# A Strassen-type output projection: one of seven split products taken as plain fp32, and its overwriting sums moved later

## The chip, the core and the metric

The kernel runs on one core of a Trainium2 chip. TensorE (PE in the profile) multiplies, VectorE (DVE), ScalarE (ACT) and GpSimd (POOL) prepare operands and empty the accumulators, SyncE (SP) issues most transfers. The metric is device time in microseconds (us) of one execution.

## The reference, cut to what matters

The reference is a decoder trunk of two layers on a sequence of 1024 vectors of 1024 features: sparse attention and a SwiGLU in layer 0, a gated MLP over chunks and a SwiGLU in layer 1. Each of the four sub-layers ends in a projection back to 1024 features that is added to the residual stream, and these four second projections are all that the change touches:

```python
return o @ w_o                                   # attention, inner size 1024
return y @ w_out                                 # gated MLP, inner size 2048
return (jax.nn.silu(h @ w_gate) * (h @ w_up)) @ w_down   # SwiGLU, inner size 2816
x = x + g1[:, None, :] * y                       # the gated residual add
```

All of it is fp32, and the comparison asks for nearly fp32 accuracy.

## The kernel before, in words

**Products.** TensorE is fed mostly with a reduced fp32 format (`float32r`). To keep accuracy every operand is split into a high part (a cast on ACT) and a low part (the difference, a subtraction on DVE or POOL), and `mm3` makes three matmuls of them: high times high, high times low, low times high (lines 176, 177 and 178). A few early projections are not split; they call `PE.matmul` on plain fp32 tiles (line 463).

**The second projection.** `out_win` computes it by Winograd's form of Strassen's scheme, seven products in place of eight. The inner dimension is cut in pieces (`[4]` for attention, `[4, 4]` for the gated MLP, `[4, 4, 3]` for each SwiGLU; a number is how many 128-wide blocks one half has). For a piece, the activations are loaded as `graw` tiles (`"1"` and `"2"`: quadrants b11, b12 and b21, b22) and the weights as `wraw` tiles (`"A"`: a11, a22; `"B"`: a12, a21). The products run in the order `ORD = (1, 2, 6, 7, 4, 5, 3)`. Product 2 multiplies a12 with b21, raw quadrants. Product 6 needs sums of quadrants: they are made in place (lines 1065, 1069, 1083, 1090), or into `gs` (line 1067) and `wsum` (line 1085), and b21 and a12 are then overwritten by their differences with those (lines 1073 and 1089). Product 4 reads the new b21 and product 3 the new a12.

**Preparing a product.** `mv_prep` and `w_prep` make four `gm` tiles and four `wst` tiles for it, each by a cast (line 1054, ACT) and a subtraction (line 1055). `GL_P` and `WL_P` give the subtraction to POOL for two of the four `gm` and for one of the four `wst`; DVE has the other five. `GS_P` gives one of four activation sums to POOL, `WS_P` two of four weight sums. A prepared product lives in four pages of the pool `pg` (37 pages, shared with everything else) and four of the eight slots of `wsp`; `wsum` has a ring of two.

**Sums out.** A product has four groups of 12 matmuls (m = 0 to 3), each in a PSUM tile `d_ps`. Products 1, 6, 7, 4 accumulate onto the same four tiles X one after the other, products 2, 5, 3 onto other tiles Z. After each group `residual` (line 949, DVE) adds the tile, scaled, into the stream `x1`; the next product on X can't start its group m before that sum of group m has read the tile.

**Order.** Each engine takes its instructions in a fixed order, which the framework's scheduler sets when the program is built, by its own estimate of durations. Code that is moved can therefore change the order of its surroundings. At the end of a SwiGLU's first half, lines 1249 and 1254 (DVE) empty the tiles of its last two products; the fourth X tile is in the PSUM slot that line 1249 frees.

Of the kernel before, what the change touches and what calls it, by code (L numbers as in the profile page):

```python
# [110 lines left out]
def trunk(ctx, tc, xT, c, modT, vec, kgb, w_idx, w_q, w_a, wuk, wuv, wo, wg, wu, wd,  # L111
# [894 lines left out]
    def out_win(src, wsrc, gate, x, pieces, xsrc=None, first=None, hook=None):  # L1006
# [39 lines left out]
        def eng(tab, i):  # L1046
            return POOL if i in tab else DVE
# [9 lines left out]

        def mv_prep(pi, j):
            n = pieces[pi]
            r = []  # L1060
            for i in range(n):
                (b11, b12), (b21, b22) = halves(pi, "1", i), halves(pi, "2", i)
                s = {1: b11, 2: b21, 7: b12, 4: b21, 5: b11, 3: b22}.get(j)
                if j == 6:
                    eng(GS_P, i).tensor_sub(b11, b12, b11)
                    s = t2("gs")
                    eng(GS_P, i).tensor_sub(s, b22, b11)
                if j == 7:
                    eng(GS_P, i).tensor_sub(b12, b22, b12)
                t = pg.tile([P, 2, CW], F32R, name="gm", tag="pg")  # L1070
                r.append(split(t, s, CW, eng(GL_P, i)))
                if j == 6:
                    eng(GS_P, i).tensor_sub(b21, b21, s)
            return r

        def w_prep(pi, j):
            n = pieces[pi] * P
            r = []
            for m in range(4):
                (a11, a22), (a12, a21) = halves(pi, "A", m, n), halves(pi, "B", m, n)  # L1080
                s = {1: a11, 2: a12, 7: a11, 4: a22, 5: a21, 3: a12}.get(j)
                if j == 6:
                    eng(WS_P, m).tensor_sub(a11, a11, a21)
                    s = tmp.tile([P, CW], F32, name="wsum", tag="wt", bufs=2)[:, :n]
                    eng(WS_P, m).tensor_sub(s, a22, a11)
                t = wsp.tile([P, 2, CW], F32R, name="wst", tag="ws")
                h, l = split(t, s, n, eng(WL_P, m))
                if j == 6:
                    eng(WS_P, m).tensor_sub(a12, a12, s)
                    eng(WS_P, m).tensor_add(a21, a21, a22)  # L1090
                r.append([(h[:, k * P:(k + 1) * P], l[:, k * P:(k + 1) * P]) for k in range(pieces[pi])])
# [5 lines left out]
        def run():  # L1097
            fetch(len(todo))
            for pi, n in enumerate(pieces):
# [7 lines left out]
                for o, j in enumerate(ORD):  # L1107
# [15 lines left out]
                    for m in range(4):  # L1123
                        p = (X if j in (1, 6, 7, 4) else Z)[m]
                        with (tc.issue_after(pe_chain[LOCK[j, m]].ins) if last and (j, m) in LOCK else ExitStack()):
                            for k in range(n):
                                mm3(p, w[m][k], mv[k], k == 0 and j in (1, 2, 5), k == n - 1 and j in (2, 3, 4), j != 2)
# [515 lines left out]
```

## Time and profile before

| what | us |
|---|---|
| time before, median of 3 runs | 2627.72 |
| lowest and highest of them | 2626.37, 2637.53 |
| profiled execution, its own time | 2638.73 |
| span of the profiled execution, first to last instruction | 2637.0 |
| TensorE busy in it | 2399.7 |
| VectorE busy in it | 2154.2 |

The profile is of one execution, whose own time is 1.7 us more than its span and 11.0 us (0.4%) above the median. Rows of a timeline give the start, the duration, the engine, line, operation, tiles and count of a merged group, and in brackets the idle time before it and what ended that. A matmul's duration overlaps that of the next one, so a matmul is priced by the distance between starts.

### The profile page before, as it was taken

How to read it: one execution, taken by the hardware profiler on the slowest of the kernel's cores; microseconds unless marked ns; L12 is line 12 of the kernel's file. 1: busy time of each engine (PE TensorE's matmuls, PEld its weight loads, DVE VectorE, ACT ScalarE, POOL GpSimd, SP SyncE). 2: the span in 40 equal slices, each digit the busy share in tenths (PEclk: the TensorE clock that was granted, in tenths of full speed). 3: DMA queues.
4: the chain of work that ended last, by engine and by line, in shares of the span. 5: the costliest groups of instructions: out<-in, count | busy, mean ns of one | idle time of the engine just before them, and what ended most of it. 6: DMA issues, size and time to landing. Idle time of an engine off the chain costs nothing.

```text
span 2637.0 us, 31201 instructions
## 1 busy us (share of the span) xinstructions
PE 2399.7 (91%) x10302; PEld 1890.6 (72%) x10302; DVE 2154.2 (82%) x3448; ACT 1223.1 (46%) x2247; POOL 1357.6 (51%) x971
## 2 busy tenths in 40 slices
PE   7979888988889999899988999988988999998996
PEld 5544577876668888777766877866766888886785
DVE  6597988798898887799979688899878656569986
ACT  5467775654523333343455454533454333333334
POOL 2131143364746655656647556575466454456663
PEclk7989889998999999999999999989999999998998
DMA  6002265634264443632022244363132222253121
GB/s 252 32 9 85 97 219 172 226 124 160 81 215 168 164 172 128 239 136 79 33 96 90 100 137 132 123 251 128 49 112 94 97 74 92 76 211 130 43 96 64
DMA packets 133921, 328.61 MB, mean 125 GB/s; under 512 B 14080, under 2 KB 30720, under 8 KB 133760
## 3 DMA queue, kind: packets, MB, share of 16 engines
q1 hardware_dynamic: 130432, 318.22, 34.4%
q0 software_dynamic: 3328, 8.39, 1.1%
q8 instruction: 82, 1.34, 0.2%
q14 instruction: 79, 0.65, 0.1%
HBM read 253.16 MB, written 73.40 MB: 124 GB/s over the span
## 4 chain that ended last, share of the span: by engine, by line
PE 48%; DVE 35%; issue 7%; DMA 5%; ACT 3%; POOL 2%; SPq 0%; DVEq 0%; ACTq 0%; POOLq 0%
PE p L1199 9%; PE p L1200 9%; PE p L1201 9%; DVE x L949 3%; DVE wst L1055 3%; PE d_ps L176 3%; PE d_ps L178 3%; PE d_ps L177 3%; DVE gm L1055 3%; DVE sc L697 2%; DVE wst L1179 2%; DVE md L243 2%; PE q_ps L463 2%; DVE ms L962 1%; PE qi_ps L403 1%
## 5 line engine op out<-in xcount | busy, mean ns | idle before, releaser
L1200 PE MATMUL p<-mv,wst 128*128 128x512 f32 x1232 | 486.5, 395 | 18.1 <-DVE mv L964 17.4
L1199 PE MATMUL p<-mv,wst 128*128 128x512 f32 x1232 | 485.6, 396 | 16.4 <-DVE uv L1234 8.1
L1201 PE MATMUL p<-mv,wst 128*128 128x512 f32 x1232 | 483.4, 393 | 0.9 <-DVE wst L1179 0.9
L1177 POOL TENSOR_TENSOR wsum<-wgu 128x512 f32<-128x512 f32 x208 | 302.9, 1457 | 321.8 <-DVE wst L1179 222.0
L176 PE MATMUL d_ps<-gm,wst 128*128 128x512 f32 x952 | 385.7, 406 | 70.4 <-DVE x L949 45.9
L178 PE MATMUL d_ps<-gm,wst 128*128 128x512 f32 x952 | 378.5, 400 | 8.0 <-POOL wst L1055 5.2
L177 PE MATMUL d_ps<-gm,wst 128*128 128x512 f32 x952 | 380.7, 400 | 0.2 <-DVE gm L1055 0.2
L1199 PEld LDWEIGHTS p<-mv,wst 128*128 128x128 f32 x1232 | 234.6, 190 | 72.8 <-DVE uv L1234 8.4
L1200 PEld LDWEIGHTS p<-mv,wst 128*128 128x128 f32 x1232 | 234.4, 190 | 73.1 <-DVE mv L964 23.7
L1178 ACT CAST wst<-wsum 128x512 fp32r<-128x512 f32 x260 | 160.8, 621 | 259.3 <-PE p L1201 109.2
L176 PEld LDWEIGHTS d_ps<-gm,wst 128*128 128x128 f32 x952 | 185.1, 195 | 122.9 <-ACT wst L1054 41.2
L1201 PEld LDWEIGHTS p<-mv,wst 128*128 128x128 f32 x1232 | 234.3, 190 | 49.8 <-DVE wst L1179 1.3
L1179 DVE TENSOR_TENSOR wst<-wsum,wst 128x512 fp32r<-128x512 f32 x208 | 206.1, 993 | 49.0 <-ACT wst L1178 48.1
L178 PEld LDWEIGHTS d_ps<-gm,wst 128*128 128x128 f32 x952 | 184.4, 194 | 51.3 <-POOL wst L1055 5.7
L949 DVE SCALAR_TENSOR_TENSOR x<-d_ps,modv,x 128x512 f32<-128x512 f32 x252 | 185.2, 740 | 37.1 <-PE d_ps L178 37.1
L177 PEld LDWEIGHTS d_ps<-gm,wst 128*128 128x128 f32 x952 | 184.9, 194 | 39.5 <-issue 1.0
L1055 POOL TENSOR_TENSOR gm<-graw,gm 128x512 fp32r<-128x512 f32 x108 | 167.5, 1562 | 73.5 <-ACT gm L1054 67.4
L1054 ACT CAST wst<-wraw 128x512 fp32r<-128x512 f32 (+1 forms) x216 | 124.2, 595 | 169.4 <-PE d_ps L178 154.9
L1055 DVE TENSOR_TENSOR wst<-wraw,wst 128x512 fp32r<-128x512 f32 (+1 forms) x162 | 148.2, 919 | 8.9 <-ACT wst L1054 8.9
L1055 POOL TENSOR_TENSOR wst<-wraw,wst 128x512 fp32r<-128x512 f32 (+1 forms) x54 | 78.5, 1453 | 143.7 <-ACT wst L1054 143.7
L1054 ACT CAST gm<-graw 128x512 fp32r<-128x512 f32 x204 | 119.0, 618 | 71.4 <-DVE wst L1055 23.0
L243 DVE SCALAR_TENSOR_TENSOR md<-md,cact 128x1024 f32<-128x1024 f32 x89 | 119.7, 1347 | 6.9 <-DMA md<-modT 6.9
(364 smaller groups left out, 5462.2 us busy)
## 6 DMA issues: line engine op xcount, KB each, us to landing
md<-modT SPq DMA_DIRECT2D x96, 512.0 KB, 4.5
wgu<-wg SPq DMA_DIRECT2D x56, 512.0 KB, 3.5
wgu<-wu SPq DMA_DIRECT2D x56, 512.0 KB, 4.4
g_d<-uv SPq DMA_DIRECT2D x88, 256.0 KB, 2.0
graw<-g_d SPq DMA_DIRECT2D x44, 512.0 KB, 7.0
wraw<-wd SPq DMA_DIRECT2D x64, 256.0 KB, 6.4
x_d<-x SPq DMA_DIRECT2D x48, 256.0 KB, 2.1
x<-x_d SPq DMA_DIRECT2D x24, 512.0 KB, 7.7
```

What stands on the lines that cost most here:

```text
L176: PE.matmul(ps, sh, mh, start=first, stop=False, skip_group_check=run)
L177: PE.matmul(ps, sh, ml, start=False, stop=False, skip_group_check=run)
L178: PE.matmul(ps, sl, mh, start=False, stop=last, skip_group_check=run)
L243: DVE.scalar_tensor_tensor(m, m, 1.0, cact, op0=ALU.mult, op1=ALU.mult, accum_out=dot)
L949: DVE.scalar_tensor_tensor(xk[:, cs], ps, gate, (xk[:, cs] if src is None else src), op0=ALU.mult, op1=ALU.add)
L1054: ACT.copy(t[:, 0, :n], s)
L1055: e.tensor_sub(t[:, 1, :n], s, f(t[:, 0, :n]))
L1177: SUM_ENG[j].tensor_tensor(s, o[0], o[1], op=o[2])
L1179: LO_ENG[j].tensor_sub(t[:, 1], s, f(t[:, 0]))
L1199: PE.matmul(ps, sh, mh, start=k == 0, stop=False)
L1200: PE.matmul(ps, sh, ml, start=False, stop=False)
L1201: PE.matmul(ps, sl, mh, start=False, stop=k == 3)
```

## The change

It touches `out_win` alone, and only the first piece (`pi == 0`) of each of the four calls. Product 2 there is made from the raw quadrants as loaded: 16 `PE.matmul` calls on fp32 tiles, one for each of four blocks k and four groups m, in place of 48 matmuls through `mm3`. Its four `gm` and four `wst` are not prepared (8 casts, 8 subtractions less). As b21 and a12 have to last until product 2 has read them, the subtractions that overwrite them stand with the preparation of product 4 and of product 3; the subtrahends, which lay in `gs` and in the ring of `wsum`, are held in four pages `hs` until then. Lines in the changed file have other numbers: 1067 is 1079, 1069 is 1081, 1073 is 1083, 1083 is 1102, 1085 is 1104, 1089 is 1106, 1249 is 1276, 1254 is 1281, and the new matmul is line 1152.

```diff
+        def hold(key):
+            w, i = key
+            if i % 2 == 0:
+                held[w] = page("hs")
+            return held[w][:, (i % 2) * CW:(i % 2 + 1) * CW]
...
         def mv_prep(pi, j):
             n = pieces[pi]
             r = []
+            if pi == 0 and j == 2:
+                return [halves(pi, "2", i)[0] for i in range(n)]
...
                 if j == 6:
                     eng(GS_P, i).tensor_sub(b11, b12, b11)
-                    s = t2("gs")
+                    s = t2("gs") if pi else hold(("g", i))
                     eng(GS_P, i).tensor_sub(s, b22, b11)
...
+                if pi == 0 and j == 4:
+                    eng(GS_P, i).tensor_sub(b21, b21, keep.pop(("g", i)))
...
-                if j == 6:
+                if j == 6 and pi == 0:
+                    keep["g", i] = s
+                elif j == 6:
                     eng(GS_P, i).tensor_sub(b21, b21, s)
...
         def w_prep(pi, j):
...
+            if pi == 0 and j == 2:
+                return [[a12[:, k * P:(k + 1) * P] for k in range(pieces[pi])]
+                        for a12, _ in (halves(pi, "B", m, n) for m in range(4))]
...
-                    s = tmp.tile([P, CW], F32, name="wsum", tag="wt", bufs=2)[:, :n]
+                    s = (tmp.tile([P, CW], F32, name="wsum", tag="wt", bufs=2) if pi else hold(("w", m)))[:, :n]
...
+                if pi == 0 and j == 3:
+                    eng(WS_P, m).tensor_sub(a12, a12, keep.pop(("w", m)))
...
                             for k in range(n):
+                                if pi == 0 and j == 2:
+                                    PE.matmul(p, w[m][k], mv[k], start=k == 0, stop=k == n - 1)
+                                    continue
                                 mm3(p, w[m][k], mv[k], k == 0 and j in (1, 2, 5), k == n - 1 and j in (2, 3, 4), j != 2)
```

DVE's order in the first SwiGLU's down projection, from the sum of product 1's first group to line 1249, before (`gs` and `graw` are sums and raw quadrants of activations, `gm_9070` is an operand of product 2):

```order
L949 SCALAR_TENSOR_TENSOR x1_8872<-d_ps_9057,modv0_98,x1_8872 128x512
L1067 TENSOR_TENSOR gs_9152<-graw_8964,graw_8854 128x512
L1067 TENSOR_TENSOR gs_9159<-graw_8938,graw_8852 128x512
L1069 TENSOR_TENSOR graw_8854<-graw_8964,graw_8854 128x512
L1073 TENSOR_TENSOR graw_8900<-graw_8900,gs_9138 128x512
L1055 TENSOR_TENSOR gm_9070<-graw_8938,gm_9070 128x512
L1083 TENSOR_TENSOR wraw_8869<-wraw_8869,wraw_8966 128x512
L1249 TENSOR_TENSOR uv_8902<-uv_8902,p6_9014 128x512
```

The same place on DVE with the change (`gm_9061` is an operand of product 6):

```order
L949 SCALAR_TENSOR_TENSOR x1_8812<-d_ps_8997,modv0_98,x1_8812 128x512
L1081 TENSOR_TENSOR graw_8794<-graw_8904,graw_8794 128x512
L1055 TENSOR_TENSOR gm_9061<-hs_9054,gm_9061 128x512
L1079 TENSOR_TENSOR hs_9065<-graw_8904,graw_8794 128x512
L1079 TENSOR_TENSOR hs_9065<-graw_8878,graw_8792 128x512
L1276 TENSOR_TENSOR uv_8842<-uv_8842,p6_8954 128x512
L1102 TENSOR_TENSOR wraw_8809<-wraw_8809,wraw_8906 128x512
```

Between the sum and the emptying of p6 there stand four instructions where there were six, and line 1083's is now behind it.

TensorE's order at the same place, before, from the end of product 1's third group to its fourth (`d_ps_9197` to `d_ps_9199` are Z tiles of product 2, `d_ps_9060` is the fourth X tile):

```order
L178 MATMUL d_ps_9059<-gm_8949,wst_8958 128x512
L176 MATMUL d_ps_9197<-gm_9061,wst_9073 128x512
L177 MATMUL d_ps_9197<-gm_9061,wst_9073 128x512
L176 MATMUL d_ps_9198<-gm_9061,wst_9076 128x512
L177 MATMUL d_ps_9198<-gm_9061,wst_9076 128x512
L176 MATMUL d_ps_9199<-gm_9061,wst_9079 128x512
L177 MATMUL d_ps_9199<-gm_9061,wst_9079 128x512
L176 MATMUL d_ps_9060<-gm_8940,wst_8961 128x512
```

With the change:

```order
L178 MATMUL d_ps_8999<-gm_8889,wst_8898 128x512
L1152 MATMUL d_ps_9101<-graw_8840,wraw_8909 128x512
L1152 MATMUL d_ps_9101<-graw_8838,wraw_8909 128x512
L1152 MATMUL d_ps_9101<-graw_8904,wraw_8909 128x512
L1152 MATMUL d_ps_9101<-graw_8878,wraw_8909 128x512
L1152 MATMUL d_ps_9102<-graw_8840,wraw_8906 128x512
L176 MATMUL d_ps_9000<-gm_8880,wst_8901 128x512
```

Six split matmuls that needed prepared operands have given way to five fp32 matmuls that need loaded tiles only; the other 11 follow product 1's fourth group.

DVE's order in front of the sum of product 6's first group (the last row of each), in the same projection, before:

```order
L1055 TENSOR_TENSOR gm_9336<-graw_8898,gm_9336 128x512
L1085 TENSOR_TENSOR wsum_9190<-wraw_8866 128x512
L949 SCALAR_TENSOR_TENSOR x1_8876<-d_ps_9200,modv0_98,x1_8876 128x512
L1055 TENSOR_TENSOR gm_9342<-graw_8938,gm_9342 128x512
L1055 TENSOR_TENSOR wst_9184<-wsum_9182,wst_9184 128x512
L1089 TENSOR_TENSOR wraw_8975<-wraw_8975,wsum_9190 128x512
L949 SCALAR_TENSOR_TENSOR x1_8872<-d_ps_9057,modv0_98,x1_8872 128x512
```

With the change:

```order
L1106 TENSOR_TENSOR wraw_8906<-wraw_8906,hs_9076 128x512
L1055 TENSOR_TENSOR wst_9147<-wraw_8803,wst_9147 128x512
L1055 TENSOR_TENSOR wst_9150<-wraw_8806,wst_9150 128x512
L949 SCALAR_TENSOR_TENSOR x1_8814<-d_ps_9103,modv0_98,x1_8814 128x512
L1083 TENSOR_TENSOR graw_8840<-graw_8840,hs_9054 128x512
L1083 TENSOR_TENSOR graw_8904<-graw_8904,hs_9065 128x512
L949 SCALAR_TENSOR_TENSOR x1_8816<-d_ps_9104,modv0_98,x1_8816 128x512
L1083 TENSOR_TENSOR graw_8878<-graw_8878,hs_9065 128x512
L1106 TENSOR_TENSOR wraw_8915<-wraw_8915,hs_9089 128x512
L1055 TENSOR_TENSOR gm_9210<-graw_8838,gm_9210 128x512
L1055 TENSOR_TENSOR gm_9218<-graw_8878,gm_9218 128x512
L949 SCALAR_TENSOR_TENSOR x1_8812<-d_ps_8997,modv0_98,x1_8812 128x512
```

The delayed subtractions (1083, 1106) still stand ahead of that sum, and so do low parts for product 7's weights (`wst_9147`, `wst_9150`) and for product 4 (`gm_9210`, `gm_9218`), while product 6's own sums and weights (the `wsum` and `wst_9184` of the list before) have moved further up.

## Rows read from the trace of the kernel before

**Rows 1.** The page of the profile: busy time of each engine with its share of the span, and the chain of work that ended last, by engine.

```profile
PE 2399.7 (91%) x10302; PEld 1890.6 (72%) x10302; DVE 2154.2 (82%) x3448; ACT 1223.1 (46%) x2247; POOL 1357.6 (51%) x971
...
PE 48%; DVE 35%; issue 7%; DMA 5%; ACT 3%; POOL 2%; SPq 0%; DVEq 0%; ACTq 0%; POOLq 0%
```

**Rows 2.** Busy time by stretches inside the first pieces of the first SwiGLU's, the gated MLP's and the second SwiGLU's projection. Columns: stretch, its length, busy time and count of PE, PE's weight loads, DVE, ACT and POOL, the granted TensorE clock as a share of 2.4 GHz, the DMA engines' share, GB/s.

```profile
1107.00:1144.00 37.00, 24.72 (x94) 18.94 (x92) 37.00 (x38) 11.73 (x21) 27.04 (x19) 0.86 0.15 59
...
1748.00:1786.00 38.00, 23.64 (x82) 17.14 (x80) 38.00 (x35) 11.05 (x21) 31.40 (x19) 0.83 0.25 96
...
2378.00:2416.00 38.00, 25.58 (x97) 19.28 (x96) 38.00 (x39) 11.94 (x22) 28.04 (x19) 0.84 0.07 28
```

**Rows 3.** Timeline of TensorE in the three first pieces: the first matmul of each SwiGLU's projection or the waits, with idle time and what ended it, and the first matmul of product 4 (the rows of 1161.13, 1803.68 and 2432.24).

```profile
1094.67 0.39 PE L176 MATMUL d_ps<-gm,wst 128*128 128x512 f32 x1
...
1110.22 0.50 PE L176 MATMUL d_ps<-gm,wst 128*128 128x512 f32 x1 [1.34 <-ACT wst L1054]
...
1117.94 0.80 PE L176 MATMUL d_ps<-gm,wst 128*128 128x512 f32 x1 [6.99 <-DVE uv L1249]
...
1142.77 0.50 PE L176 MATMUL d_ps<-gm,wst 128*128 128x512 f32 x1 [3.46 <-ACT wst L1054]
...
1161.13 0.39 PE L176 MATMUL d_ps<-gm,wst 128*128 128x512 f32 x1
...
1756.44 0.79 PE L178 MATMUL d_ps<-gm,wst 128*128 128x512 f32 x1 [5.24 <-POOL wst L1055]
...
1785.84 0.80 PE L176 MATMUL d_ps<-gm,wst 128*128 128x512 f32 x1 [6.39 <-DVE x L949]
...
1803.68 0.39 PE L176 MATMUL d_ps<-gm,wst 128*128 128x512 f32 x1
...
2389.61 0.80 PE L176 MATMUL d_ps<-gm,wst 128*128 128x512 f32 x1 [6.99 <-DVE uv L1249]
...
2414.46 0.80 PE L176 MATMUL d_ps<-gm,wst 128*128 128x512 f32 x1 [3.97 <-ACT wst L1054]
...
2432.24 0.39 PE L176 MATMUL d_ps<-gm,wst 128*128 128x512 f32 x1
```

**Rows 4.** Busy time and granted clock (third column from the end) of stretches behind such waits, and of one full product (1150.3 to 1161.1). Columns as in Rows 2.

```profile
1117.90:1124.10 6.20, 6.16 (x15) 4.86 (x16) 6.20 (x7) 3.62 (x6) 4.20 (x4) 0.50 0.00 0
...
1144.70:1148.10 3.40, 3.40 (x10) 2.61 (x9) 3.40 (x4) 1.66 (x4) 2.49 (x2) 0.50 0.00 0
1150.30:1161.10 10.80, 10.80 (x49) 8.97 (x48) 10.80 (x14) 4.66 (x8) 4.51 (x4) 1.00 0.90 313
...
1756.40:1765.80 9.40, 8.39 (x19) 6.12 (x20) 9.40 (x9) 1.59 (x3) 9.40 (x6) 0.50 0.10 37
...
1785.80:1789.70 3.90, 3.86 (x9) 3.09 (x10) 3.90 (x5) 3.63 (x7) 1.99 (x2) 0.50 0.00 0
```

**Rows 5.** Timeline of DVE in the first SwiGLU's projection: a low part of product 2 (1103.93), the sum of product 1's first group (1106.82), the rows up to line 1249, and the sum of product 6's first group (1144.45).

```profile
1103.93 1.78 DVE L1055 TENSOR_TENSOR gm<-graw,gm 128x512 fp32r<-128x512 f32 x1
...
1106.82 0.74 DVE L949 SCALAR_TENSOR_TENSOR x<-d_ps,modv,x 128x512 f32<-128x512 f32 x1
1107.48 3.13 DVE L1067 TENSOR_TENSOR gs<-graw 128x512 f32<-128x512 f32 x2
1110.54 1.75 DVE L1069 TENSOR_TENSOR graw<-graw 128x512 f32<-128x512 f32 x1
1112.21 1.74 DVE L1073 TENSOR_TENSOR graw<-graw,gs 128x512 f32<-128x512 f32 x1
...
1117.21 0.68 DVE L1249 TENSOR_TENSOR uv<-uv,p 128x512 f32<-128x512 f32 x1
...
1144.45 0.74 DVE L949 SCALAR_TENSOR_TENSOR x<-d_ps,modv,x 128x512 f32<-128x512 f32 x1
```

**Rows 6.** Timeline of DVE, then of POOL, in the same projection: two DVE subtractions one behind the other while POOL was idle (its idle time of 2.48 us ends at 1128.82), and the POOL subtraction behind them.

```profile
1127.40 0.68 DVE L1085 TENSOR_TENSOR wsum<-wraw 128x512 f32<-128x512 f32 x1
1128.00 0.68 DVE L1090 TENSOR_TENSOR wraw<-wraw 128x512 f32<-128x512 f32 x1
...
1128.82 1.62 POOL L1055 TENSOR_TENSOR wst<-wsum,wst 128x512 fp32r<-128x512 f32 x1 [2.48 <-ACT wst L1054]
```

**Rows 7.** Plain fp32 matmuls of an early projection (16 calls for each of 8 heads): the group, and 27 of its records in one stretch of the timeline; then two split matmuls of a SwiGLU, 56 records apart in an unbroken run.

```profile
L463 PE MATMUL q_ps<-h,wq 128*128 128x512 f32 x256 | 114.0, 593 | 0.0
...
264.70 11.75 PE L463 MATMUL q_ps<-h,wq 128*128 128x512 f32 x27
...
2279.75 0.39 PE L1200 MATMUL p<-mv,wst 128*128 128x512 f32 x1
...
2292.44 0.39 PE L1199 MATMUL p<-mv,wst 128*128 128x512 f32 x1
```

**Rows 8.** Timeline of DVE in the gated MLP's projection: the sums of product 1's second group and of product 6's first group.

```profile
1748.45 0.74 DVE L949 SCALAR_TENSOR_TENSOR x<-d_ps,modv,x 128x512 f32<-128x512 f32 x1
...
1785.06 0.74 DVE L949 SCALAR_TENSOR_TENSOR x<-d_ps,modv,x 128x512 f32<-128x512 f32 x1
```

**Rows 9.** Timeline of the attention's projection: TensorE's wait at the end of the attention, DVE's emptying of attention scores that stands before it, and the first row of a dot product (line 243) that fills DVE there.

```profile
557.15 0.39 PE L177 MATMUL o_ps<-rgpT,rgv 128*128 128x256 f32 x1 [1.95 <-POOL sqp L1104]
...
556.43 0.28 DVE L187 TENSOR_TENSOR rgpT<-pt_ps,rgpT 128x128 fp32r<-128x128 f32 x1
...
567.75 2.31 DVE L243 SCALAR_TENSOR_TENSOR md<-md,cact 128x1024 f32<-128x1024 f32 x1
```

More of the change, by code (lines that the diff above doesn't have):

```diff
@@ L1056, in split @@
             return t[:, 0], t[:, 1]
+        held = {}
+        def hold(key):
[3 more added lines that the diff above has]
+            return held[w][:, (i % 2) * CW:(i % 2 + 1) * CW]
+        keep = {}
         def mv_prep(pi, j):
@@ L1088, in w_prep @@
                 if j == 6:
-                    eng(WS_P, m).tensor_sub(a12, a12, s)
+                    if pi == 0:
+                        keep["w", m] = s
+                    else:
+                        eng(WS_P, m).tensor_sub(a12, a12, s)
                     eng(WS_P, m).tensor_add(a21, a21, a22)
```

## The prediction

> **What bounds the kernel now.** I read the page first: TensorE is busy for 91% of the span, but the chain that ended last lies 48% on TensorE and 35% on DVE [rows 1]. So a stage has to be read for itself. The change touches the first pieces of four second projections. In three of them, windows over some 37 us show DVE busy for the whole window while TensorE works for about two thirds of it, at a granted clock of 0.83 to 0.86 [rows 2]. There DVE sets the pace.
>
> TensorE's timeline says which DVE instruction each wait hangs on [rows 3]. In the first SwiGLU it waits 1.34 us for a cast, 6.99 us for line 1249 (product 1's fourth tile isn't free) and 3.46 us inside product 6, for a cast that comes behind a `wsum` of its third group, which DVE made late. The second SwiGLU repeats this 1271.7 us later (6.99 and 3.97 us). The gated MLP waits 5.24 us for a POOL subtraction inside product 2 and 6.39 us inside product 6 (the view names line 949, which ends just before; the place is the same third group). Behind each such wait the granted clock is 0.50 (1.2 GHz) for 3.4 to 9.4 us [rows 4], so a wait costs itself and half of the half-clock stretch behind it: 6.2, 3.4, 9.4 and 3.9 us give 3.1, 1.7, 4.7 and 2.0 us. Products 7 and 4 follow unbroken at 10.8 us each [rows 4], so product 7 started at about 1150.3, 1792.9 and 2421.4. From product 4 on TensorE runs without such waits to the end of the piece, and I measure the change by when product 4 starts: 1161.13, 1803.68 and 2432.24 us [rows 3].
>
> **The change part by part.** *Matmuls.* A plain fp32 call of the same shape is two records (256 for 128 calls), and 27 records last 11.75 us, 0.435 each: 0.87 us a call. Split matmuls start every 12.69/56 = 0.227 us, so the three they replace take 0.68 us [rows 7]. 16 calls cost 16 × 0.19 = 3.0 us more a piece, 12 us over four, and this is the price where TensorE is the bound. Where it waits for DVE anyway, the waits hide it.
>
> The rows price one call at 0.87 us because it leaves two records of 0.435 us. The Trainium skill's page "FP8 and Floating Point Precision", section TensorE Precision Notes, says true FP32 takes four passes through the array. By that rule a call would be an estimated 4 × 0.227 = 0.91 us, and the four pieces would lose 14.5 us instead of 12.
>
> *Preparation.* A piece loses eight casts on ACT, which is 46% busy [rows 1] and isn't late, and eight subtractions, five on DVE and three on POOL. An SBUF-only DVE subtraction starts 0.60 us behind the one before it while POOL idles, but takes 1.74 to 1.78 us when POOL works beside it [rows 5, 6]. Line 949, which reads PSUM, takes 0.74 us in each row [rows 5, 8]. So five removed subtractions are worth 3.0 to 8.7 us of DVE.
>
> The rows show a DVE subtraction between SBUF tiles nearly three times as long beside POOL as without it, and line 949 not. The Trainium skill, "SBUF — State Buffer", section Who interferes with whom, says that a DVE instruction with two SBUF inputs contends with a GpSimd instruction that reads SBUF, one with at most one such input not. If so, each POOL subtraction less frees DVE too, which speaks for the change: three a piece at an estimated 1.1 us would give at most 3 us more than I count.
>
> *What moves.* The eight delayed subtractions stay, five on DVE. The order puts them behind product 2's groups, and again ahead of the sum of product 6's first group. This decides: product 7 can't start until that sum is done, and DVE reaches it after a queue of rows. In the first SwiGLU the queue between the sums of the first groups of product 1 and product 6 holds 38 DVE instructions before and 38 after, 28 of them SBUF-only in both, because low parts for products 7 and 4 have moved ahead. I take its length as before: 1144.45 − 1106.82 = 37.6 us [rows 5], 1.11 us a row less the sums.
>
> *First SwiGLU.* The low part of 1.78 us at 1103.93 is gone, so product 1's first sum stands at 1106.82 − 1.7 = 1105.1. Four rows instead of six lead to line 1249: 1112.6, where it was 1117.21 [rows 5]. TensorE has five fp32 calls (4.3 us) for the same time, from about 1107.9, so the waits of 1.34 and 6.99 us and the half clock behind them go. Then come 12 × 0.227 = 2.7 us of product 1 and 11 × 0.87 = 9.6 us: product 2 ends at about 1125, and product 6 (one product is 10.8 us [rows 4]) at about 1136. What is late next is product 6's first sum, at 1105.1 + 37.6 = 1142.7, done at 1143.4. TensorE idles some 7 us there, in front of product 7, in place of the 3.46 inside product 6, whose `wsum` now comes in time. I take 2.5 us for the half clock behind it, between 1.7 and 3.1, since the wait is as long as that at line 1249. Product 4 starts at 1143.4 + 10.8 + 2.5 = 1156.7 against 1161.13: **4.4 us** gained.
>
> *Second SwiGLU.* The same order, rows and durations give **3.7 us**, less because the clock there stood at 0.50 for shorter before.
>
> *Gated MLP.* The wait for POOL's 5.24 us goes: product 2 needs no low parts. But product 6's first sum comes 36.6 us after product 1's second [rows 8], the rows between are about as many, and it starts 0.6 us earlier: 1784.5, done at 1785.2. Then 10.8 + 2.0: product 4 at 1798.1 against 1803.68, **5.6 us** gained (product 7 starts where product 6's third group started before, so that half of product 6 no longer lies behind DVE's queue).
>
> *Attention.* Its projection begins behind the scores. TensorE waits 1.95 us there [rows 9] for a POOL row, itself slowed by product 2's preparation on DVE and POOL, which moves away: about 4 us, down to 0 if those waits are something else. But DVE then waits for the fp32 product 2, because the first delayed subtraction (b21's) is queued ahead of product 6's low parts, and the fp32 calls are 3 us slower. Between these I count 42 us of DVE work from there to product 7, as many as behind the dot product at 567.75 [rows 9] before. I take a loss of 1 us; bounds are 3 us gained and 5 lost.
>
> *Sum.* 4.4 + 3.7 + 5.6 − 1 = 12.7 us. Nothing gives it back later: from product 4 to the next piece TensorE is the bound, and raw tiles of the next piece load as early as before or earlier. The profiled execution took 2638.73 us; 2638.73 − 12.7 = 2626.0. The median lies at 2627.72/2638.73 = 0.9958 of it, so **2615 us**, a gain of 0.5%.
>
> **The rivals.** *B: DVE doesn't hold it.* The removed subtractions and the quieter POOL shorten the queue by 7 us or more, product 7 doesn't wait, and all waits go with their half clocks: 1.34 + 6.99 + 3.46 and 4.8 (3.1 + 1.7) less 3.0 is 13.6 us in the first SwiGLU, 13 in the second, 11.6 + 6.7 − 3.0 = 15.3 in the gated MLP. With nothing lost in the attention that is 42 us: 2586; halfway, 2600. For it: 8.7 us is the upper bound for five subtractions. Against it: DVE is full over the whole window [rows 2], and its queue is no shorter by count.
>
> *C: the gain is eaten.* The waits move in front of product 7 at their full length with a longer half clock, and the fp32 calls cost their 12 us where TensorE bounds. Each piece then ends where it did or 3 us later: 2628 to 2640. For it: my own sum has a wait of 7 us there that wasn't there before.
>
> *D: slower.* Product 6's first sum stands behind the delayed subtractions and low parts for later products. If POOL reads SBUF throughout, each of the 28 SBUF-only rows takes 1.74 us instead of about 1.1: 28 × 1.74 + 6.5 (the other ten rows) = 55 us, product 7 at about 1161 in place of 1150.3 and product 4 13 us late with the half clock; twice that and 6 us in the gated MLP, whose queue is shorter by such rows, give 32 us: 2638.7 + 32 = 2671, on the median's scale 2660. It decides from about 1.27 us a row, where the gain of 4.4 us is used up (28 × 0.16). Against it: POOL was busy for 27 us of 37 there [rows 2], and loses three subtractions.
>
> **How the numbers follow.** My forecast, A (2607 to 2623), has 0.52; B 0.16, C 0.20, D 0.12. A measurement of this kernel can tell 0.5% (13 us) from no change, so the bound is 2614.6, and A lies half on either side. Faster: 0.26 + 0.16 = 0.42. Same: 0.26 + 0.20 = 0.46. Slower: 0.12. The range goes from B's halfway point, 2600, to C's end, 2639: that leaves out D and half of B, 0.20.
>
> **What would show it.** Right: the 6.99 us wait for p6's emptying is gone in both SwiGLUs, and so is the one inside product 6 on a cast behind `wsum`. In their place product 7 waits 6 to 7 us for DVE's sum (line 949). Product 4 starts about 62 us after the projection's first matmul, where it took 66.5 from 1094.67. An fp32 call is two records of 0.43 us; the windows of DVE are still full. Wrong: product 6's first sum lies over 3 us from 1105.1 + 37.6 on this scale (the count of rows was then a bad measure of the queue); product 4 gains but the next piece starts no earlier; or the attention's projection moves by more than 5 us.

## The result, and the profile after

| what | us |
|---|---|
| time after, median of 5 runs (lowest and highest) | 2614.86 (2610.54, 2617.94) |
| time before beside it, median of 5 runs | 2627.72 (2625.63, 2637.53) |
| ratio after/before, 95% interval | 0.9933 [0.9917, 0.9949] |
| a second series, ratio | 0.9914 [0.9892, 0.9936] |
| profiled execution, its span | 2608.8 |

The two medians differ by 12.9 us, which is the forecast's 12.7; by the ratios, with their intervals, the kernel is faster by 17.6 us (13.4 to 21.8) and, in the second series, by 22.7 us (16.9 to 28.5). The median after stands where the prediction put it (2615), but the gain is probably larger than its 12.7 us: in the later series the kernel before had medians of 2630.9 to 2635.0 us, so 2627.72 lies 3 to 7 us low.

The page of the profile after: TensorE's busy time as before [rows 1], in a span 28 us shorter.

```profile
PE 2401.8 (92%) x10238; PEld 1873.6 (72%) x10238; DVE 2122.4 (81%) x3428; ACT 1206.6 (46%) x2215; POOL 1341.3 (51%) x959
```

TensorE's timeline after, which answers to [rows 3]: first matmul of each of the three projections, runs of plain fp32 records and product 6's first matmul (1115.02) in the first SwiGLU, the long wait of each first piece, and product 4's first matmul (1145.44, 1783.17, 2404.46).

```profile
1085.80 0.39 PE L176 MATMUL d_ps<-gm,wst 128*128 128x512 f32 x1
...
1098.94 4.45 PE L1152 MATMUL d_ps<-graw,wraw 128*128 128x512 f32 x10
...
1105.98 9.60 PE L1152 MATMUL d_ps<-graw,wraw 128*128 128x512 f32 x22
...
1115.02 0.79 PE L176 MATMUL d_ps<-gm,wst 128*128 128x512 f32 x1
...
1132.54 0.76 PE L176 MATMUL d_ps<-gm,wst 128*128 128x512 f32 x1 [6.04 <-DVE x L949]
...
1145.44 0.39 PE L176 MATMUL d_ps<-gm,wst 128*128 128x512 f32 x1
...
1723.68 0.63 PE L176 MATMUL d_ps<-gm,wst 128*128 128x512 f32 x1
...
1769.84 0.77 PE L176 MATMUL d_ps<-gm,wst 128*128 128x512 f32 x1 [5.38 <-DVE x L949]
...
1783.17 0.39 PE L176 MATMUL d_ps<-gm,wst 128*128 128x512 f32 x1
...
2344.29 0.39 PE L176 MATMUL d_ps<-gm,wst 128*128 128x512 f32 x1
...
2391.20 0.77 PE L176 MATMUL d_ps<-gm,wst 128*128 128x512 f32 x1 [6.20 <-DVE x L949]
...
2404.46 0.39 PE L176 MATMUL d_ps<-gm,wst 128*128 128x512 f32 x1
```

The waits for line 1249 and for POOL are gone, and so is the wait of several us inside product 6; in the gated MLP 0.80 us for a cast are left there. One long wait remains in each first piece, in front of product 7, for line 949: product 6's first sum. Product 4 starts 59.6, 59.5 and 60.2 us after the first matmul, where it took 66.5, 67.6 and 65.9 us before: [rows 3] with the first matmuls of the gated MLP's and the second SwiGLU's projection before,

```profile
1736.05 0.40 PE L176 MATMUL d_ps<-gm,wst 128*128 128x512 f32 x1
...
2366.33 0.39 PE L176 MATMUL d_ps<-gm,wst 128*128 128x512 f32 x1
```

Windows after, over the same stretches as [rows 2] and behind the three waits as [rows 4]:

```profile
1096.00:1132.50 36.50, 30.49 (x106) 19.58 (x104) 36.50 (x41) 11.72 (x21) 26.06 (x17) 0.96 0.18 73
1738.00:1770.00 32.00, 25.81 (x84) 15.31 (x83) 32.00 (x33) 11.54 (x21) 24.00 (x15) 0.97 0.19 75
2355.00:2391.00 36.00, 30.00 (x104) 19.15 (x102) 36.00 (x40) 11.80 (x21) 24.43 (x16) 0.98 0.10 38
...
1132.50:1136.90 4.40, 4.37 (x11) 3.48 (x12) 4.03 (x6) 3.25 (x6) 3.12 (x3) 0.53 0.10 16
1770.00:1774.00 4.00, 4.00 (x10) 3.14 (x11) 3.98 (x4) 1.31 (x3) 2.20 (x3) 0.50 0.13 39
2391.20:2395.20 4.00, 4.00 (x10) 3.13 (x11) 3.63 (x5) 3.25 (x6) 2.72 (x3) 0.50 0.03 6
```

DVE is still busy for every microsecond of the three long stretches; that it also sets the pace there is shown below, by late and pad. Its timeline after, in the first SwiGLU's projection, answers to [rows 5]:

```profile
1096.25 0.74 DVE L949 SCALAR_TENSOR_TENSOR x<-d_ps,modv,x 128x512 f32<-128x512 f32 x1
...
1102.10 0.68 DVE L1276 TENSOR_TENSOR uv<-uv,p 128x512 f32<-128x512 f32 x1
...
1124.96 0.74 DVE L949 SCALAR_TENSOR_TENSOR x<-d_ps,modv,x 128x512 f32<-128x512 f32 x1
1125.63 1.28 DVE L1083 TENSOR_TENSOR graw<-graw,hs 128x512 f32<-128x512 f32 x2
1126.83 0.74 DVE L949 SCALAR_TENSOR_TENSOR x<-d_ps,modv,x 128x512 f32<-128x512 f32 x1
1127.49 1.36 DVE L1083 TENSOR_TENSOR graw<-graw,hs 128x512 f32<-128x512 f32 x1
1128.77 1.75 DVE L1106 TENSOR_TENSOR wraw<-wraw,hs 128x512 f32<-128x512 f32 x1
1130.45 1.28 DVE L1055 TENSOR_TENSOR gm<-graw,gm 128x512 fp32r<-128x512 f32 x2
1131.65 0.74 DVE L949 SCALAR_TENSOR_TENSOR x<-d_ps,modv,x 128x512 f32<-128x512 f32 x1
```

Product 6's first sum (the last row) stands behind delayed subtractions (lines 1083, 1106) and low parts for product 4, none of which product 7 needs.

### The profile page after: what moved, and what is told of

It is laid out like the page before. It is cut to its first block, busy times and chain, and to the rows that moved or that the text cites. A ratio compares the mean times of both kernels' runs of the same rounds, so it can differ in the third digit from the quotient of the medians.

```text
span 2608.8 us, 30989 instructions
## 1 busy us (share of the span) xinstructions
PE 2401.8 (92%) x10238; PEld 1873.6 (72%) x10238; DVE 2122.4 (81%) x3428; ACT 1206.6 (46%) x2215; POOL 1341.3 (51%) x959
## 5 line engine op out<-in xcount | busy, mean ns | idle before, releaser
L1227 PE MATMUL p<-mv,wst 128*128 128x512 f32 x1232 | 485.5, 394 | 17.3 <-DVE mv L964 16.3
L176 PE MATMUL d_ps<-gm,wst 128*128 128x512 f32 x888 | 362.8, 409 | 59.9 <-DVE x L949 53.8
L177 PE MATMUL d_ps<-gm,wst 128*128 128x512 f32 x888 | 356.0, 401 | 0.0
L178 PE MATMUL d_ps<-gm,wst 128*128 128x512 f32 x888 | 353.9, 400 | 0.6 <-DVE wst L1055 0.6
L176 PEld LDWEIGHTS d_ps<-gm,wst 128*128 128x128 f32 x888 | 172.6, 194 | 109.9 <-ACT wst L1054 45.4
L178 PEld LDWEIGHTS d_ps<-gm,wst 128*128 128x128 f32 x888 | 172.5, 194 | 39.5 <-DVE wst L1055 1.5
L177 PEld LDWEIGHTS d_ps<-gm,wst 128*128 128x128 f32 x888 | 172.8, 195 | 37.1 <-issue 1.9
L1055 POOL TENSOR_TENSOR gm<-graw,gm 128x512 fp32r<-128x512 f32 x100 | 153.7, 1547 | 80.7 <-ACT gm L1054 76.2
L1054 ACT CAST wst<-wraw 128x512 fp32r<-128x512 f32 (+1 forms) x200 | 114.9, 593 | 164.4 <-PE d_ps L178 149.8
L1054 ACT CAST gm<-graw 128x512 fp32r<-128x512 f32 x188 | 110.4, 618 | 97.0 <-DVE graw L1083 27.8
L1055 DVE TENSOR_TENSOR wst<-wraw,wst 128x512 fp32r<-128x512 f32 (+1 forms) x150 | 133.7, 895 | 8.3 <-ACT wst L1054 8.3
L1205 ACT CAST wst<-wgu 128x512 fp32r<-128x512 f32 x104 | 64.5, 620 | 133.2 <-PE p L1228 73.0
```

The costliest lines, as they stand in the source:

```text
L176: PE.matmul(ps, sh, mh, start=first, stop=False, skip_group_check=run)
L177: PE.matmul(ps, sh, ml, start=False, stop=False, skip_group_check=run)
L178: PE.matmul(ps, sl, mh, start=False, stop=last, skip_group_check=run)
L1054: ACT.copy(t[:, 0, :n], s)
L1055: e.tensor_sub(t[:, 1, :n], s, f(t[:, 0, :n]))
L1205: ACT.copy(t[:, 0], s)
```

## The experiments

One table first. Each ratio is to runs of the kernel before made in the same series, so it is not the quotient of two medians of the table. The projections' lengths go from a projection's first matmul to its last in the profiled execution; "attention" goes from a mark among the matmuls of the attention that all kernels share (495 us in the kernel before, ahead of the attention's projection) to the first SwiGLU projection's first matmul.

| kernel | median us | ratio to before [95%] | attention | 1st SwiGLU | gated MLP | 2nd SwiGLU |
|---|---|---|---|---|---|---|
| before | 2627.72 | | 599.7 | 251.3 | 188.5 | 251.4 |
| before_again | 2631.80 | 0.9994 [0.9981, 1.0007] | 595.9 | 252.3 | 189.0 | 251.7 |
| after | 2614.86 | 0.9933 [0.9917, 0.9949] | 597.7 | 247.0 | 178.7 | 245.3 |
| after_again | 2613.43 | 0.9914 [0.9892, 0.9936] | 598.2 | 245.1 | 178.3 | 245.1 |
| no_attention | 2612.69 | 0.9919 [0.9906, 0.9932] | 594.9 | 244.3 | 180.2 | 245.4 |
| only_gmlp | 2624.92 | 0.9964 [0.9948, 0.9979] | 596.1 | 252.3 | 181.8 | 251.9 |
| delay_alone | 2642.37 | 1.0030 [1.0016, 1.0043] | 599.2 | 254.2 | 181.6 | 253.1 |
| prep_kept | 2638.07 | 1.0016 [1.0004, 1.0029] | 600.7 | 250.7 | 185.7 | 252.0 |
| dve_kept | 2634.56 | 1.0009 [0.9996, 1.0022] | 599.0 | 252.4 | 182.6 | 249.3 |
| pool_kept | 2616.53 | 0.9934 [0.9916, 0.9952] | 596.3 | 246.4 | 179.4 | 245.6 |
| pad | 2610.40 | 0.9913 [0.9898, 0.9929] | 595.9 | 244.7 | 180.0 | 245.6 |
| late | 2600.99 | 0.9880 [0.9865, 0.9895] | 594.3 | 241.8 | 176.1 | 242.3 |
| late_all | 2606.86 | 0.9911 [0.9896, 0.9926] | 594.6 | 241.7 | 178.5 | 241.9 |
| late_noatt | 2602.96 | 0.9878 [0.9854, 0.9901] | 594.4 | 241.4 | 177.0 | 241.9 |

**How large, and where: before_again, after_again, no_attention, only_gmlp.** The first two repeat the two kernels. The others apply the change to some calls only:

```diff
+        raw2 = ('o' if xsrc is not None else 'y' if len(pieces) == 2 else 'g') in 'yg'
...
-            if pi == 0 and j == 2:
+            if pi == 0 and j == 2 and raw2:
```

(`'yg'` in no_attention, `'y'` in only_gmlp, and `raw2` at every place where the change asks for the first piece.)

> The kernel before, unchanged, for a second profile. Theory: the 10 us by which the two profiles differ at the start of the attention's projection (538.28 against 528.02 us) belong to the one profiled execution, so here that projection starts at 528 to 532 us and the span is 2622 to 2630 us; inside the projections nothing moves: product 4 starts 66.5 us (first SwiGLU), 67.6 (gated MLP) and 65.9 us (second SwiGLU) after the projection's first matmul, each within 0.5. Rival: the change itself sped up the stages ahead of the projection; then the projection starts at 537 to 539 us again.

> The changed kernel, unchanged, beside late_noatt on one chip, for the size of the gain and a second profile. Theory by the projections' lengths in the traces so far (6, 8.5 and 6 us, nothing in the attention): ratio 0.991 to 0.993, 18 to 23 us. Rival, the terms of the prediction: 12.7 us, ratio 0.995. Product 4 starts 59 to 60, 59 to 61 and 60 to 61 us after the projection's first matmul by the first, 62, 62 and 62 us by the second.

> The change in the SwiGLUs and the gated MLP only; the attention's projection is as before. Theory: the attention's projection lost some 1.4 us by the change (10.3 us ahead at its start, 8.9 us ahead at the next projection), so this takes 1 to 2 us less than the changed kernel: 2613 to 2614 us, ratio 0.9925 to 0.9945. Rival: the delayed subtractions and the dearer fp32 matmuls cost the attention 5 us or more: 2610 us or less. Other rival: the attention gained and gave the others room: 2620 us.

> The change in the gated MLP's projection only. Theory by the traces: it gained 9.7 of the 18 us that the four projections gained between the two profiles, more than the 5.6 us of the prediction: 2617 to 2620 us. Rival, the terms of the prediction: 5.6 us, 2622 us. Its projection ends 178.7 us after its first matmul by the first, 183 us by the second (188.5 before).

The kernel before, profiled again, reached the mark 6.2 us earlier (its span of 2632.9 us is still 3 us above the expected 2622 to 2630), and its three projections had the same lengths within 1 us: of the 28 us between the two first profiles, about 7 are the one execution's and lie ahead of the change. Over the kernels with and without it, the change takes 6.5 us from the first SwiGLU's projection (252.0 to 245.5, three executions each), 9.0 from the gated MLP's (188.75 in two executions to 179.75 in four) and 6.4 from the second SwiGLU's (251.7 to 245.3): 21.9 us, at the upper end of what the first ratio allows and inside the second's interval. In the attention's stage five executions without the change took 594.4 to 599.7 us and the two of the changed kernel 597.7 and 598.2 (pad and late below, whose edits leave the attention out, 595.9 and 594.3): no difference that the spread of 5 us can show, and no_attention's ratio doesn't differ from the changed kernel's either. Inside that stage two things move against each other, as the prediction had it: in these four executions the projection starts 39.8 to 41.0 us after the mark and takes 105.7 to 107.3 us, in the five without the change 40.5 to 43.3 and 101.5 to 104.7. only_gmlp gained 9.5 us (5.5 to 13.7): its interval holds both the 7 us by which its projection is shorter and the 9.0.

**Does DVE's queue set product 7: late.** The preparations for products 4, 5 and 3 may not stand ahead of product 6's first sum on DVE; nothing is left out.

```diff
         def prep(pi, j):
             if pi < len(pieces) and (pi, j) not in pre:
-                pre[pi, j] = (mv_prep(pi, j), w_prep(pi, j))
+                with (tc.issue_after(first6[0].ins) if pi == 0 and j in (4, 5, 3) and first6 else ExitStack()):
+                    pre[pi, j] = (mv_prep(pi, j), w_prep(pi, j))
...
-                        residual(p, x[m + mo], ch, gate[:, m + mo:m + mo + 1])
+                        r = residual(p, x[m + mo], ch, gate[:, m + mo:m + mo + 1])
+                        if pi == 0 and j == 6 and m == 0 and xsrc is None:
+                            first6.append(r)
```

> The changed kernel, but in the SwiGLUs and the gated MLP DVE's preparations for products 4, 5 and 3 of the first piece (with the delayed subtractions) are queued behind the sum of product 6's first group. Theory: that sum waits for DVE's queue, and product 7 for the sum; about seven rows of 1 to 1.7 us leave the queue, the waits of 6.4, 5.4 and 6.6 us in front of product 7 shrink to under 1 us and the half clock behind them goes: 6 to 8 us for each projection, 2591 to 2597 us in all. Rival 1: something else holds product 7 (its own operands, a tile): the wait stays and the time is 2615 us. Rival 2: the wait moves to product 4, whose operands are now late: 2607 to 2620 us with waits of 4 us or more in front of product 4 or inside it.

The windows from product 1's first sum to product 6's in the first SwiGLU, of the changed kernel and then of late (columns as in [rows 2]):

```profile
1096.25:1131.65 35.40, 30.24 (x105) 19.37 (x103) 35.40 (x39) 11.62 (x21) 24.96 (x17) 0.97 0.18 72
```

```profile
1094.03:1123.45 29.42, 29.42 (x103) 19.02 (x102) 29.42 (x33) 8.93 (x16) 21.66 (x14) 1.00 0.22 88
```

The queue is shorter by 6.0 us, TensorE is busy throughout at a clock of 1.00, and product 7 starts without a wait of note, 40.8 us after the first matmul (46.7 before this edit). DVE's and TensorE's timelines of late (line 1086 is the changed kernel's 1083; the third of the sums at 1122.13 is product 6's first; the first matmuls of the projection and of product 7 are at 1083.57 and 1124.33):

```profile
1122.13 2.05 DVE L949 SCALAR_TENSOR_TENSOR x<-d_ps,modv,x 128x512 f32<-128x512 f32 x3
1124.11 1.88 DVE L1086 TENSOR_TENSOR graw<-graw,hs 128x512 f32<-128x512 f32 x3
```

```profile
1083.57 0.39 PE L176 MATMUL d_ps<-gm,wst 128*128 128x512 f32 x1
...
1124.33 0.47 PE L176 MATMUL d_ps<-gm,wst 128*128 128x512 f32 x1
...
1128.60 0.47 PE L176 MATMUL d_ps<-gm,wst 128*128 128x512 f32 x1 [1.29 <-ACT gm L1057]
...
1137.08 0.47 PE L176 MATMUL d_ps<-gm,wst 128*128 128x512 f32 x1 [2.09 <-DVE x L949]
```

About half of the 6 us comes back as short waits in product 7 and behind it (rival 2 in part), and half is kept, so the time lies above the 2591 to 2597 us expected. By the medians late takes 12 to 14 us less than the changed kernel, by the ratios 9 to 14; the three projections together give 8 to 11 of them (660.2 us after 671.0 and 668.5), and the rest is within the spread of the other stretches.

**Is TensorE the bound: pad.**

```diff
                                 if pi == 0 and j == 2:
                                     PE.matmul(p, w[m][k], mv[k], start=k == 0, stop=k == n - 1)
+                                    if k == 1 and xsrc is None:
+                                        PE.matmul(p, w[m][k], mv[k], start=False, stop=False)
                                     continue
```

> The changed kernel with four more plain fp32 matmuls (block 1 a second time in each group) in product 2 of the SwiGLUs and the gated MLP, 3.5 us each; it counts that block twice in the output. Theory (DVE's queue sets product 7, TensorE idles 5.4 to 6.6 us in front of it): the waits there shrink to about 2 to 3 us, product 7 starts where it did, 46 to 48 us after the projection's first matmul, and the time is 0 to 3 us above the changed kernel, ratio 0.993 to 0.995. Rival (TensorE's work sets the pace, so that fp32's higher price is paid in full): product 7 starts 3.5 us later in each, ratio 0.997.

TensorE's timeline of pad (first matmul of the first SwiGLU's projection, product 6's first, then the waits in front of product 7 in the first SwiGLU and the gated MLP):

```profile
1087.82 0.39 PE L176 MATMUL d_ps<-gm,wst 128*128 128x512 f32 x1
...
1120.48 0.79 PE L176 MATMUL d_ps<-gm,wst 128*128 128x512 f32 x1
...
1134.83 0.47 PE L176 MATMUL d_ps<-gm,wst 128*128 128x512 f32 x1 [2.88 <-DVE x L949]
...
1767.91 0.77 PE L176 MATMUL d_ps<-gm,wst 128*128 128x512 f32 x1 [4.25 <-DVE x L949]
```

In the first SwiGLU product 6 starts 32.7 us after the first matmul in place of 29.2, and product 7 at 47.0 in place of 46.7: the wait swallowed the added 3.5 us. In the other two product 7 starts 0.8 and 1.0 us later, with waits of 4.25 and 3.77 us left, and the time didn't rise. So the fp32 price, which is less than what was added, is hidden in these three projections, as the prediction had it.

**Which half of the change gains: delay_alone, prep_kept.** delay_alone takes out the three places that make product 2 of raw tiles; prep_kept has the plain matmuls but makes the parts all the same:

```diff
-            if pi == 0 and j == 2:
-                return [halves(pi, "2", i)[0] for i in range(n)]
...
                     mv, w = pre[pi, j]
+                    if pi == 0 and j == 2:
+                        mv = [halves(pi, "2", i)[0] for i in range(n)]
+                        w = [[a12[:, k * P:(k + 1) * P] for k in range(n)]
+                             for a12, _ in (halves(pi, "B", m, n * P) for m in range(4))]
```

> The second half of the change alone: the overwriting subtractions are delayed and their subtrahends held in pages, but product 2 is split and prepared as before. By its order line 1249's emptying moves ahead of product 1's first sum in the first SwiGLU, and product 6's first sum is the 41st row behind that (38th before and with the change); in the gated MLP it is the 39th (32nd before, 33rd with the change). Theory (rows removed from DVE's queue are what counts): 2 us gained in each SwiGLU, some 5 us lost in the gated MLP, ratio 0.997 to 1.003. Rival (the delay, or the freed rings of gs and wsum, is what gains): ratio 0.992 to 0.995.

> The changed kernel, with product 2's plain fp32 matmuls, but its high and low parts are still made (8 casts, 8 subtractions for each projection) and not used. Theory (DVE's removed rows carry the gain): product 6's first sum is the 42nd row behind product 1's in the first SwiGLU (38th with the change), 37th in the gated MLP (33rd); product 7 starts 4 to 6 us later than with the change in each, and some 7 us of the gain are left: ratio 0.996 to 0.998. Rival (that TensorE has matmuls which need no prepared operand is the gain): ratio 0.992 to 0.994, product 7 where the change has it.

TensorE's timeline in the first SwiGLU's projection, of delay_alone and then of prep_kept (with its first matmul):

```profile
1121.39 0.79 PE L178 MATMUL d_ps<-gm,wst 128*128 128x512 f32 x1 [4.82 <-DVE wst L1055]
...
1138.06 0.79 PE L176 MATMUL d_ps<-gm,wst 128*128 128x512 f32 x1 [4.41 <-ACT wst L1054]
...
1155.06 0.76 PE L176 MATMUL d_ps<-gm,wst 128*128 128x512 f32 x1 [4.12 <-DVE x L949]
```

```profile
1090.04 0.39 PE L176 MATMUL d_ps<-gm,wst 128*128 128x512 f32 x1
...
1124.36 0.79 PE L176 MATMUL d_ps<-gm,wst 128*128 128x512 f32 x1 [4.09 <-ACT wst L1054]
...
1128.07 0.80 PE L178 MATMUL d_ps<-gm,wst 128*128 128x512 f32 x1 [2.06 <-DVE wst L1055]
...
1143.15 0.47 PE L176 MATMUL d_ps<-gm,wst 128*128 128x512 f32 x1 [2.48 <-DVE x L949]
```

In the SwiGLUs neither half gains by itself. With the delay alone line 1249's wait goes too, but the same time is waited inside products 2 and 6 and in front of 7. With the unused parts product 7 starts 53.1 us after the first matmul, 6.4 later than with the change, and the gain is gone. Both expectations missed in size: delay_alone had the signs the wrong way round (2 us lost in each SwiGLU, 7 gained in the gated MLP), and prep_kept kept nothing of the 7 us that I had left to it. In the gated MLP the rival is right: there the delay alone makes the projection 7.1 us shorter, most of the 9.0. The late `wsum` of product 6 [rows 3], freed from its ring of two by the pages, may be what the delay mends there; no run separates the pages from the delay, so that stays open. The projections of delay_alone together are 3.5 us shorter than before on the mean, and its time is longer all the same: what it loses lies in other stretches.

**Whose removed work: pool_kept, dve_kept.** Of product 2's unused parts, those are still made whose low part was POOL's (3) or DVE's (5).

```diff
             if pi == 0 and j == 2:
+                for i in range(n):
+                    if eng(GL_P, i) is POOL:
+                        split(pg.tile([P, 2, CW], F32R, name="gm", tag="pg"), halves(pi, "2", i)[0], CW, POOL)
                 return [halves(pi, "2", i)[0] for i in range(n)]
...
             if pi == 0 and j == 2:
+                for m in range(4):
+                    if eng(WL_P, m) is POOL:
+                        split(wsp.tile([P, 2, CW], F32R, name="wst", tag="ws"), halves(pi, "B", m, n)[0], n, POOL)
```

> The changed kernel, but the parts of product 2 whose low part was POOL's are still made (3 casts and 3 POOL subtractions for each projection) and not used; DVE's queue between product 1's and product 6's first sums keeps its 38 rows in the SwiGLUs. Theory (three POOL subtractions less also shorten DVE's rows: the queue took 35.4 us where the prediction took the 37.6 of before): product 7 starts 2 to 3 us later than with the change, 48.7 to 49.7 us after the projection's first matmul in the SwiGLUs, ratio 0.993 to 0.996. Rival (POOL's load is nothing to DVE, the queue was shorter for its other rows): 46.7 us as with the change, ratio 0.991 to 0.993.

> The complement: of product 2's unused parts only those are still made whose low part was DVE's (5 casts and 5 DVE subtractions for each projection). DVE's queue between the two sums has 40 rows in the SwiGLUs (38 with the change) and about two rows more ahead of it. Theory: product 7 starts 3.5 to 5 us later than with the change, 50 to 52 us in the SwiGLUs, and with pool_kept's delay this makes up the 6.4 us of prep_kept; ratio 0.995 to 0.998. Rival (the removed DVE subtractions are cheap, 0.6 us each, and POOL's share is the gain): at most 2 to 3 us later, 49 us, ratio 0.992 to 0.994.

The window from product 1's first sum to product 6's, of pool_kept and then of dve_kept:

```profile
1102.80:1141.40 38.60, 31.99 (x106) 20.57 (x105) 38.60 (x39) 12.83 (x23) 29.71 (x20) 0.91 0.18 69
```

```profile
1108.50:1148.10 39.60, 32.21 (x100) 20.35 (x98) 39.60 (x41) 12.69 (x24) 26.20 (x17) 0.89 0.13 53
```

With three POOL subtractions more and as many rows (38, and the one that closes the window; one emptying of a PSUM tile has given way to one more sum of SBUF tiles), DVE took 38.6 us in place of 35.4. Its SBUF-only rows took 1.13 us on the mean in place of 1.03, which is 2.6 of the 3.2 us, for three POOL instructions that DVE doesn't wait for by any operand. In the changed kernel's window the 11 SBUF-only rows that POOL didn't touch took 0.60 us each from start to start, and the 14 that took 1.02 to 1.70 us all ran beside a POOL instruction. Product 7 started 3.0 us later, as expected. The time hardly moved, since this time the wait stood earlier, and product 4 came only 1.0 us later (60.7 after 59.6):

```profile
1129.48 0.79 PE L178 MATMUL d_ps<-gm,wst 128*128 128x512 f32 x1 [6.61 <-DVE wst L1055]
...
1142.32 0.47 PE L176 MATMUL d_ps<-gm,wst 128*128 128x512 f32 x1 [0.70 <-DVE x L949]
```

(TensorE of pool_kept.) With the five DVE subtractions product 7 starts 5.4 us later, above the expected 3.5 to 5, and the ratio shows no gain. Its gated MLP and second SwiGLU are still 6 and 2 us shorter than before; what took these 8 us elsewhere stays open. The two delays make 8.4 us, not the 6.4 of prep_kept; the order of instructions is another in each, so they needn't add up. In the SwiGLUs, then, both POOL's and DVE's removed subtractions move product 7, and with DVE's made again hardly any of the gain is left.

**The attention: late_all, late_noatt.** late_all drops `and xsrc is None` from late; late_noatt is late with no_attention's `raw2`.

> As late, and in the attention's projection too the delayed subtractions and the preparations for products 4, 5 and 3 are queued behind the sum of product 6's first group. In the trace of late TensorE waits there 4.65 and 1.21 us inside product 6, for operands whose sums stand on DVE behind three delayed subtractions of 0.69 to 1.74 us. Theory (what stands ahead in DVE's queue sets these waits): they shrink to under 2 us in all, 4 to 6 us less than late with the half clock: 2595 to 2597 us, ratio 0.9855 to 0.987. Rival: DVE's other work there (the dot products of line 243, the squares) fills the same time: 2600 to 2602 us, ratio 0.988. Other rival: product 4 of the attention is then late: 2603 us or more.

> late in the SwiGLUs and the gated MLP, and the attention's projection as in the kernel before. Theory: the change is worth nothing in the attention (from a mark at 495 us to the next projection it took 596 to 598 us with and 595 to 600 us without it), so this is within 4 us of late: 2597 to 2605 us, ratio 0.986 to 0.990. Rival 1: the attention's 16 dearer matmuls and its delayed subtractions cost what the medians of no_attention and the changed kernel differ by, 2 to 4 us or more: ratio 0.985 or less. Rival 2: the gain of late hangs on the attention's change: ratio 0.992 or more.

TensorE's timeline of the attention's projection, of the changed kernel and of late_all, and DVE's of late_all (line 1109 is the changed kernel's 1106):

```profile
565.61 0.79 PE L176 MATMUL d_ps<-gm,wst 128*128 128x512 f32 x1 [4.60 <-ACT wst L1054]
```

```profile
565.42 0.50 PE L176 MATMUL d_ps<-gm,wst 128*128 128x512 f32 x1 [1.19 <-ACT wst L1057]
...
585.43 0.79 PE L176 MATMUL d_ps<-gm,wst 128*128 128x512 f32 x1 [5.34 <-DVE x L949]
```

```profile
577.77 1.72 DVE L1086 TENSOR_TENSOR graw<-graw,hs 128x512 f32<-128x512 f32 x2
...
580.08 1.28 DVE L1109 TENSOR_TENSOR wraw<-wraw,hs 128x512 f32<-128x512 f32 x2
...
584.63 0.74 DVE L949 SCALAR_TENSOR_TENSOR x<-d_ps,modv,x 128x512 f32<-128x512 f32 x1
```

The wait inside product 6 shrinks as expected and stands inside product 7 instead; the stage is as long as in late (594.6 and 594.3 us). So nothing is gained, as the rival had it, but not only for its reason: of the 6.9 us of DVE's rows ahead of the sum that this wait ends with, 3.4 are the moved subtractions themselves, 1.7 a square and 1.7 a low part. That late_all took 6 us more than late overall is not the attention's: in its profile 2.4 us lie in the gated MLP's projection and 3.6 in the stretch ahead of that, which no edit touches and which differs as much between two executions of the kernel before (last section). late_noatt equals late within their intervals (some 6 us), so the change shows no worth in the attention. late and late_noatt beat both kernels.

## Why the prediction came out as it did

- **The waits that go, and the one that comes: right.** Measured from the projection's first matmul, product 1's first sum stood at 10.45 us (predicted 1105.1 − 1094.67 = 10.4), line 1249 (now 1276) at 16.3 (17.9; before 22.5 [rows 5]), product 6 started at 29.2 (30.3), and product 7 waited 6.04, 5.38 and 6.20 us for line 949 (6 to 7; the gated MLP's is shorter). Product 6's first sum stood at 45.9 where 48.0 was forecast, inside the 3 us that the prediction allowed. late shows that DVE's queue holds it, pad that TensorE doesn't.
- **The step that was mis-sized: "I take its length as before", 37.6 us.** The queue took 35.4, and the gain at product 4 is 6.8 us where 4.4 were forecast; the second SwiGLU gained 5.7 in place of 3.7. The count of rows, 38 and 38, was right; a row got shorter, (35.4 − 6.5)/28 = 1.03 us in place of 1.11. The prediction had noted that each POOL subtraction less frees DVE as well, and left it outside the sum. pool_kept puts its price at 2.6 to 3.2 us for three. The Trainium skill, "SBUF — State Buffer", section Who interferes with whom, says that a DVE instruction with two SBUF inputs contends with a GpSimd instruction that reads SBUF; this window agrees, with 0.60 us for a row that POOL doesn't touch and up to 1.70 beside it. In the gated MLP the same term of the sum was short: product 6's first sum stood 45.3 us after the first matmul, where 48.5 were forecast, and product 4 came 8.1 us earlier in place of 5.6. There the delay alone brings most of the gain (delay_alone), which the sum did not count by itself.
- **The half clock:** 2.5 us assumed; 12.90 us from product 7 to product 4, less 10.88 for a product at the full clock, is 2.0 in the first SwiGLU, 2.5 (where 2.0 were assumed) and 2.4 in the others.
- **fp32's price: right.** Two records start 0.43 us apart, 0.86 us a call, hidden by the wait (pad). The Trainium skill, "FP8 and Floating Point Precision", section TensorE Precision Notes, counts four passes for true FP32, which would give an estimated 4 × 0.227 = 0.91 us; the trace has a little less.
- **The attention: no loss to be seen** where 1 us was forecast; the runs can't tell 0 from 1. An earlier start and a longer projection are both there.
- **The chances:** by the ratios the gain lies beyond 0.5%, on the side to which 0.42 was given. Rival B's halfway point, 2600, is what late reaches by taking rows out of the queue. C fell with pad, D with rows of 1.03 us where it needed 1.27.

By the terms the forecast is 12.7 of about 20 us. That 2615 was met is luck in part: the gain was taken some 8 us too small, and the median of before that it was scaled to was 3 to 7 us low.

## What to carry to other kernels

Where one engine is busy for the whole of a stretch, count its queue in rows between the two instructions that TensorE waits for, and price a row by what runs beside it: here work taken from POOL shortened DVE's rows too. A dearer matmul that needs no preparation cost nothing here, since the wait behind it was longer than its extra time. Then look for rows in that queue that are not needed yet: moving them behind the awaited one gave another 9 to 14 us here.

## What the runs showed that I had not expected

Stretches that no edit touches differ by several us between executions of one kernel: in the two of the kernel before, the mark at 495 us was passed 6.2 us apart, and the stretch between the first SwiGLU's and the gated MLP's projections took 390.1 and 393.8 us. Over all kernels the mark was passed 6.9 us earlier (after) to 5.0 us later (delay_alone) than in the first profile, and that stretch took 388.4 us (pad) to 396.7 (delay_alone); whether the edits have a part in that wider spread is not shown. A difference of 5 us between two profiles says little unless it lies inside one of the three edited projections, where two executions of one kernel agreed within 2 us.
